# Convolution sums and inversion products in PSUM, gates on ScalarE, a shorter reciprocal root

## The chip, the cores and the metric

The kernel runs on one core of one Trainium2 chip. Its engines are TensorE (PE, with weight loads shown apart as PEld), VectorE (DVE), ScalarE (ACT), GpSimd (POOL) and SyncE (SP), which here issues DMAs; ACT issues some too. The metric is the device time of one execution in microseconds, lower is better. A run is one number; the median of several is what counts, and one execution has been recorded as a profile.

## What is computed

One encoder layer with four head groups, on two requests of 2048 tokens by 1024 features (`r` = 0 and 1) with shared weights. Cut to what matters here:

```python
def gdn_chunked(q, k, v, g, beta):              # chunks of 64 tokens, 32 of them
    l_mat = where(strict, einsum(k_beta, k) * decay, 0)
    sol = triangular_solve(eye + l_mat, rhs, lower=True, unit_diagonal=True)
    ...                                         # a scan over 32 chunks, state 64x64 per head

def gdn_branch(qkv, gates, conv_w, ...):
    act = silu(centred_dwconv(qkv, conv_w))     # 5 taps along the sequence, one filter a channel
    q, k, v = split(act, 3)
    q, k = l2_norm(q) * HEAD_DIM ** -0.5, l2_norm(k)
    ...                                         # forward and backward scan, then rms_norm

def encoder_layer(x, mem, ...):
    proj = rms_norm(x, pre_g) @ w_in
    y_a = fourier_mix(a_u, w_fnet) * silu(a_z)
    y_b = gdn_branch(b_qkv, b_gates, ...) * silu(b_z)
    y_c = neighbourhood_attn(cq, ck, cv, rpb) * silu(c_z)
    y_d = memory_attn(d_q, rms_norm(mem, mem_g), w_mem_kv) * silu(d_z)
    out = concatenate([y_a, y_b, y_c, y_d]) @ w_out
    return x + rms_norm(out, post_g)
```

## The kernel before

Products are made from pairs of 16-bit parts, three matmuls each (L484 to L486, L494 to L496, L500 to L502 are the three of one product). `build` issues the stages and gives each a band of priority; a scheduler then writes each engine's list from the bands and the dependences, with a timing model of its own, so that stages overlap. Within an engine the list is run in order.

- **Projections** (`pass_a`, `pass_b`, `pass_z`, band 0): blocks of 256 tokens are normed (`xblock`), transposed through memory (`xT`), and multiplied by the columns of `w_in` into the PSUM tile `pj`, two banks called `mm`. `pass_a` makes q, k, v for the convolution, stored as `braw`, and the gates: ACT copies 256 columns of a `pj`, and DVE copies its last 16, scaled (L569).
- **gdn_pre** (band 3): for each request and each of 8 blocks of 256 tokens, `conv_pair` runs for k, q and v, 48 pairs in all. It loads `craw`, and for each half (128 channels) ACT writes the first tap (L889) and DVE adds the other four (L891), all in the SBUF tile `cacc`; ACT makes the tanh (L893), and DVE the product (L894). ACT and POOL then split it into two parts for PE. `norms` makes the reciprocal norms of q and k by `rsqrt`. `gdn_pair` multiplies chunks (PSUM tiles `p`, of which DVE makes `kt` at L1005, `lt` and `mt` at L1013) and stores the records `rec`.
- **gdn_sub(0)**, then **gdn_sub(1)** (band 1): triangular inversions by 31 steps in two directions `d`, on two diagonal blocks `b`. Each step makes a product `pr` (L1056) and adds it to `T` (L1059); DVE does b = 1, POOL b = 0, both in SBUF. Then blocks are combined on PE (`px`, `pz`).
- **gdn_chain** (bands 1 and 1.5): the 32 steps of the scan. PE's products are called `pc` and `pw`; SP loads `rA` and others ahead of each step; `gdn_out` stores `yb`.
- **fnet** (band 2): for each request a butterfly on DVE (L1331 to L1334), DFT products on PE (`pdf`, PSUM banks `s` and `t`), and features (`pfy` on PE, `Y` on DVE at L1434 and L1438).
- **mem_attn**, then **na_attn** (band 2): memory attention, and neighbourhood attention in 64 iterations, with scores in banks `s` and `t`, transposes by DMA (`nPT`, L1639), values `pno`, stores `yc` (L1666).
- **pass_o**: the output projection `po`, 8 blocks for each request; `prep` loads `yb`, the others' results and the gate path `oz`, and DVE and POOL multiply.

PSUM has eight banks: two `mm`; `s`, `t`, `o` (pool `pat`); `ga`, `gq`, `as` (pool `pgd`, the delta rule's). SBUF pools on the right belong to gdn_pre, gdn_sub(0), gdn_sub(1) and the chain in turn, so these run one after the other.

`rsqrt` (L232) is a bit trick (a shift, L239, and a multiply-add on integers, L240) and three Newton steps of three operations (L243, L244, L245), all small and on DVE. It serves the norms of x, of q and k, of the gdn output, of the memory and of the output.

The lines of the convolution:

```python
acc = pp.tile([P, 2, CB], F32, name=self.nm("cacc"), tag="cacc", bufs=2)
for f in range(2):
    w = self.cws[:, 2 * i + f]
    nc.scalar.activation(acc[:, f], raw[:, f, 0:CB], AF.Copy, scale=w[:, 0:1])
    for t in range(1, 5):
        nc.vector.scalar_tensor_tensor(out=acc[:, f], in0=raw[:, f, t:t + CB], ...)
```

## Time and profile before

| | |
|---|---|
| runs, us | 2514.59, 2507.51, 2510.41; median 2510.41 |
| profiled execution | 2511.93 us, span from first to last instruction 2510.2 us |
[...]
| busy over the span | PE 2008.5 us (80%), DVE 1935.1 (77%), ACT 1153.7 (46%), POOL 1059.3 (42%) |
| instructions | PE 23715, DVE 4693, ACT 2530, POOL 1149 |
| DMA | 476.07 MB, 190 GB/s on average |

A share over the whole span is an average over stages with different limits. The page's slices, the busy time by stage, the waits and the single groups of instructions say more; they are in the section of rows below. An operation is named by its line in the kernel before (L891); in `out<-in` stand the names of the tiles. A wait is put down to the engine and line that released it last.

### The profile page before, as it was taken

Reading aid. Unit: us, or ns where it says so; the run is one execution under the profiler, and the core shown is the slowest. Engines: PE = TensorE matmul, PEld = TensorE weight load, DVE = VectorE, ACT = ScalarE, POOL = GpSimd, SP = SyncE. Lnnn points to the kernel's source line nnn. Section 1 sums busy time; section 2 is a strip of 40 time slices with the busy share of each in tenths; the row PEclk is TensorE's granted clock in tenths of the full one; section 3 lists DMA queues with packets and bytes.
Section 4 is the critical chain, followed back from the end, with each engine's and each line's share of the span. In section 5 each row is a group of like instructions: output and inputs, shape, how many; then the busy total and the mean of one; then the engine's idle time right before and its main releaser. Section 6 shows DMA issues by size and latency. Waiting matters only on the chain. (4 is left out here: it accounts for less than half of the span.)

```text
span 2510.2 us, 60051 instructions
## 1 busy us (share of the span) xinstructions
PE 2008.5 (80%) x23715; PEld 1711.6 (68%) x23715; DVE 1935.1 (77%) x4693; ACT 1153.7 (46%) x2530; POOL 1059.3 (42%) x1149
## 2 busy tenths in 40 slices
PE   0787778787446776899688998878877899899998
PEld 0565667666335665687566787767766888788887
DVE  3579998989999979767987857767577756677764
ACT  1455544553354421345166755657566644332322
POOL 1236665445476667613853422222223343433320
PEclk9988899887757998899899998999989999999999
DMA  9899999999745695499789987999999984555543
GB/s 89 185 203 192 205 237 234 240 205 231 170 111 145 172 226 127 110 243 181 156 178 224 213 210 214 217 194 206 231 181 231 218 264 139 172 185 184 189 158 118
DMA packets 827483, 476.07 MB, mean 190 GB/s; under 512 B 556864, under 2 KB 789952, under 8 KB 818752
## 3 DMA queue, kind: packets, MB, share of 16 engines
q1 hardware_dynamic: 802624, 438.67, 76.5%
q10 hardware_dynamic: 24576, 33.56, 4.5%
q8 instruction: 186, 3.05, 0.5%
q14 instruction: 97, 0.79, 0.1%
HBM read 243.38 MB, written 163.73 MB: 162 GB/s over the span
## 5 line engine op out<-in xcount | busy, mean ns | idle before, releaser
L484 PE MATMUL pj<-xT,w 128*128 128x256 f16 x2592 | 739.2, 285 | 131.6 <-DVE st L213 42.5
L486 PE MATMUL pj<-xT,w 128*128 128x256 f16 x2592 | 737.2, 284 | 4.5 <-POOL w L421 4.5
L485 PE MATMUL pj<-xT,w 128*128 128x256 f16 x2592 | 738.2, 285 | 0.0
L485 PEld LDWEIGHTS <-w 128*128 128x128 f16 x2592 | 264.6, 102 | 114.0 <-issue 74.5
L484 PEld LDWEIGHTS <-w 128*128 128x128 f16 x2592 | 264.2, 102 | 106.4 <-issue 32.1
L486 PEld LDWEIGHTS <-w 128*128 128x128 f16 x2592 | 264.5, 102 | 53.8 <-POOL w L421 10.5
L500 PE MATMUL po<-w,oy 128*128 128x256 f16 x1024 | 280.6, 274 | 0.8 <-ACT oy L715 0.8
L502 PE MATMUL po<-w,oy 128*128 128x256 f16 x1024 | 280.1, 274 | 1.4 <-DVE oy L716 1.4
L501 PE MATMUL po<-w,oy 128*128 128x256 f16 x1024 | 280.7, 274 | 0.0
L891 DVE SCALAR_TENSOR_TENSOR cacc<-craw,cws,cacc 128x256 f32<-128x256 f32 x384 | 241.5, 663 | 7.2 <-ACT cacc L889 5.9
L494 PE MATMUL pj<-w,xT 128*128 128x272 f16 (+1 forms) x512 | 153.5, 300 | 41.6 <-ACT st L561 23.2
L230 POOL TENSOR_TENSOR oy<-oy,oz 128x512 f32<-128x512 f32 x60 | 100.7, 1699 | 189.2 <-ACT oy L701 178.2
L1165 POOL COPY bk<-rA 64x512 f16<-64x512 f16 x124 | 84.8, 684 | 224.9 <-PE pw L502 167.1
L765 ACT ACTIVATE oj<-po,wsc_o 128x256 f32<-128x256 f32 x128 | 59.5, 470 | 244.3 <-PE po L502 244.3
L421 POOL TENSOR_TENSOR w<-wt,w 128x512 f16<-128x512 f32 (+1 forms) x70 | 85.9, 1236 | 172.6 <-ACT w L419 150.5
L495 PE MATMUL pj<-w,xT 128*128 128x272 f16 (+1 forms) x512 | 153.8, 301 | 0.8 <-POOL w L421 0.8
L496 PE MATMUL pj<-w,xT 128*128 128x272 f16 (+1 forms) x512 | 153.6, 300 | 0.0
L500 PE MATMUL pno<-nPT,nv 128*128 128x64 f16 x704 | 78.6, 200 | 62.1 <-DMA nPT<-np__2821_27987 25.3
L1172 ACT ACTIVATE b<-rA 64x1536 f16<-64x1536 f16 x64 | 92.7, 1475 | 53.0 <-PE pc L1133 30.5
L227 POOL TENSOR_TENSOR km<-kt,km 128x256 f16<-128x256 f32 x128 | 95.2, 765 | 39.3 <-ACT km L1009 37.4
L502 PEld LDWEIGHTS <-oy 128*128 128x128 f16 x1024 | 100.6, 98 | 13.7 <-DVE oy L716 1.8
L500 PEld LDWEIGHTS <-oy 128*128 128x128 f16 x1024 | 100.6, 98 | 13.0 <-ACT oy L715 0.9
(443 smaller groups left out, 6153.5 us busy)
## 6 DMA issues: line engine op xcount, KB each, us to landing
xT<-xTd SPq DMA_DIRECT2D x32, 1024.0 KB
rec<-km SPq DMA_DIRECT2D x32, 768.0 KB
rA<-rec SPq DMA_DIRECT2D x64, 384.0 KB
xTd<-xT SPq DMA_DIRECT2D x16, 1024.0 KB
sz<-st ACTq DMA_DIRECT2D x64, 256.0 KB
oz<-sz SPq DMA_DIRECT2D x16, 1024.0 KB
out_dram<-oo SPq DMA_DIRECT2D x32, 512.0 KB
craw<-braw SPq DMA_DIRECT2D x48, 260.0 KB
```

Of the source, the lines that this page charges most:

```text
L227: self.nc.gpsimd.tensor_tensor(out=out, in0=a, in1=b, op=ALU.subtract)
L230: self.nc.gpsimd.tensor_tensor(out=out, in0=a, in1=b, op=ALU.mult)
L484: nc.tensor.matmul(ps, whi, xhi, start=(kt == 0), stop=False)
L485: nc.tensor.matmul(ps, whi, xlo, start=False, stop=False)
L486: nc.tensor.matmul(ps, wlo, xhi, start=False, stop=(kt == KT - 1))
L494: nc.tensor.matmul(ps, xhi, whi, start=(kt == 0), stop=False)
L495: nc.tensor.matmul(ps, xhi, wlo, start=False, stop=False)
L496: nc.tensor.matmul(ps, xlo, whi, start=False, stop=(kt == KT - 1))
L500: nc.tensor.matmul(ps, whi, xhi, start=start, stop=False)
L501: nc.tensor.matmul(ps, whi, xlo, start=False, stop=False)
L502: nc.tensor.matmul(ps, wlo, xhi, start=False, stop=stop)
L891: nc.vector.scalar_tensor_tensor(out=acc[:, f], in0=raw[:, f, t:t + CB], scalar=w[:, t:t + 1], in1=acc[:, f], op0=ALU.mult, op1=ALU.add)
```

## The change

Four edits.

1. The convolution's sums live in a PSUM tile `pcv`, in the banks `s` and `t` in turn (a counter `ncv`); `cacc` in SBUF holds only the result of the product after the tanh.
2. In the inversions the product of b = 1, DVE's, goes to a PSUM tile `pq` in bank `as`; POOL's stays in `pr`. A switch `SPLITADD` that was always on is gone.
3. The scaled copy of the gates is made by ACT.
4. `rsqrt` has 8 operations for 11: one integer operation for two, one Newton step of three, and one step of a higher order of four.

```diff
@@ -148,7 +148,6 @@
 PSS = ("s", "t")
 PSV = ("o", "o")
 SUB = 1
-SPLITADD = lambda k: True
 
 
 class Kern:
@@ -173,6 +172,7 @@
         self.D = {}
         self.prio = {}
         self.xbufs = 2
+        self.ncv = 0
         self.zh = {}
 
     def nm(self, s):
@@ -236,13 +236,17 @@
         n = x.shape[-1]
         y = self.tt([P, n], tag=f"rq{n}", bufs=4)
         t = self.tt([P, n], tag=f"rt{n}", bufs=4)
-        nc.vector.tensor_scalar(out=y.bitcast(I32), in0=x.bitcast(I32), scalar1=1, scalar2=None, op0=ALU.logical_shift_right)
-        nc.vector.tensor_scalar(out=y.bitcast(I32), in0=y.bitcast(I32), scalar1=-1.0, scalar2=float(0x5F3759DF),
-                                op0=ALU.mult, op1=ALU.add)
-        for i in range(3):
-            eng.scalar_tensor_tensor(out=t, in0=y, scalar=-0.5, in1=y, op0=ALU.mult, op1=ALU.mult)
-            eng.scalar_tensor_tensor(out=t, in0=t, scalar=1.0, in1=x, op0=ALU.mult, op1=ALU.mult)
-            eng.scalar_tensor_tensor(out=(out if i == 2 else y), in0=t, scalar=1.5, in1=y, op0=ALU.add, op1=ALU.mult)
+        stt = lambda o, a, s, b, op: eng.scalar_tensor_tensor(out=o, in0=a, scalar=s, in1=b, op0=op, op1=ALU.mult)
+        nc.vector.tensor_scalar(out=y.bitcast(I32), in0=x.bitcast(I32), scalar1=-0.5, scalar2=float(0x5F3759DF), op0=ALU.mult, op1=ALU.add)
+        stt(t, y, -0.5, y, ALU.mult)
+        stt(t, t, 1.0, x, ALU.mult)
+        stt(y, t, 1.5, y, ALU.add)
+
+        c = math.sqrt(0.375)
+        stt(t, y, c, y, ALU.mult)
+        stt(t, t, 1.0, x, ALU.mult)
+        stt(t, t, -1.25 / c, t, ALU.add)
+        stt(out, t, 1.875, y, ALU.add)
 
     def consts(self):
         nc, I = self.nc, self.I
@@ -566,7 +570,7 @@
                 ps = self.pmm.tile([P, 512], F32, name=self.nm("pj"), tag="mm")
                 self.mm_tok(ps[:, 0:272], W["ag"], 272, xT, t * P)
                 nc.scalar.activation(st[:, t], ps[:, 0:256], AF.Copy, scale=2.0 ** -19)
-                nc.vector.tensor_scalar(out=self.gates[r][:, 2 * tb + t, :], in0=ps[:, 256:272], scalar1=d, scalar2=None, op0=ALU.mult)
+                nc.scalar.activation(self.gates[r][:, 2 * tb + t, :], ps[:, 256:272], AF.Copy, scale=d)
             nc.scalar.dma_start(D[f"au{r}"][:, 2 * tb:2 * tb + 2, :], st)
 
         def between(tb):
@@ -883,15 +887,18 @@
         i = "qkv".index(u)
         raw = pp.tile([P, 2, CB + 4], F32, name=self.nm("craw"), tag="craw", bufs=2)
         nc.sync.dma_start(raw, self.D[f"braw{r}"][:, 2 * i:2 * i + 2, tb * CB:tb * CB + CB + 4])
-        acc = pp.tile([P, 2, CB], F32, name=self.nm("cacc"), tag="cacc", bufs=2)
+
+        pcv = self.pat.tile([P, 2, CB], F32, name=self.nm("pcv"), tag="st"[self.ncv % 2])
+        self.ncv += 1
         for f in range(2):
             w = self.cws[:, 2 * i + f]
-            nc.scalar.activation(acc[:, f], raw[:, f, 0:CB], AF.Copy, scale=w[:, 0:1])
+            nc.scalar.activation(pcv[:, f], raw[:, f, 0:CB], AF.Copy, scale=w[:, 0:1])
             for t in range(1, 5):
-                nc.vector.scalar_tensor_tensor(out=acc[:, f], in0=raw[:, f, t:t + CB], scalar=w[:, t:t + 1], in1=acc[:, f], op0=ALU.mult, op1=ALU.add)
+                nc.vector.scalar_tensor_tensor(out=pcv[:, f], in0=raw[:, f, t:t + CB], scalar=w[:, t:t + 1], in1=pcv[:, f], op0=ALU.mult, op1=ALU.add)
+        acc = pp.tile([P, 2, CB], F32, name=self.nm("cacc"), tag="cacc", bufs=2)
         e = pp.tile([P, 2, CB], F32, name=self.nm("cexp"), tag="cexp", bufs=2)
-        nc.scalar.activation(e, acc, AF.Tanh, scale=self.cinv[:, i:i + 1])
-        nc.vector.scalar_tensor_tensor(out=acc, in0=e, scalar=1.0, in1=acc, op0=ALU.add, op1=ALU.mult)
+        nc.scalar.activation(e, pcv, AF.Tanh, scale=self.cinv[:, i:i + 1])
+        nc.vector.scalar_tensor_tensor(out=acc, in0=e, scalar=1.0, in1=pcv, op0=ALU.add, op1=ALU.mult)
         if u == "v":
             dst = [self.vt[:, :, l].rearrange("p n f c -> p f n c") for l in range(2)]
         else:
@@ -1044,21 +1051,19 @@
                 nc.gpsimd.memset(T[d], 0.0)
                 nc.gpsimd.memset(T[d].rearrange("p b i j -> p b (i j)")[:, :, 0:1024:33], 1.0)
             pr = tl([P, 2, 2, 256], F32, "pr")
+            pq = self.pgd.tile([P, 2, 256], F32, name=self.nm("ppr"), tag="as")
 
             for k0 in range(31):
                 for d in range(2):
                     k = k0 if d == 0 else 31 - k0
                     js, is_ = (slice(k + 1, 32), slice(0, k + 1)) if d == 0 else (slice(0, k), slice(k, 32))
                     nj, ni = js.stop - js.start, is_.stop - is_.start
-                    pv = pr[:, d, :, 0:nj * ni].rearrange("p b (j i) -> p b j i", j=nj)
+                    pv = [t.rearrange("p (j i) -> p j i", j=nj) for t in (pr[:, d, 0, 0:nj * ni], pq[:, d, 0:nj * ni])]
                     for b in range(2):
                         eng = nc.vector if b == 1 else nc.gpsimd
-                        eng.tensor_tensor(out=pv[:, b], in0=lp[d][:, b, k, js].unsqueeze(2).to_broadcast([P, nj, ni]),
+                        eng.tensor_tensor(out=pv[b], in0=lp[d][:, b, k, js].unsqueeze(2).to_broadcast([P, nj, ni]),
                                           in1=T[d][:, b, k, is_].unsqueeze(1).to_broadcast([P, nj, ni]), op=ALU.mult)
-                        if SPLITADD(k0):
-                            eng.tensor_tensor(out=T[d][:, b, js, is_], in0=T[d][:, b, js, is_], in1=pv[:, b], op=ALU.add)
-                    if not SPLITADD(k0):
-                        nc.vector.tensor_tensor(out=T[d][:, :, js, is_], in0=T[d][:, :, js, is_], in1=pv, op=ALU.add)
+                        eng.tensor_tensor(out=T[d][:, b, js, is_], in0=T[d][:, b, js, is_], in1=pv[b], op=ALU.add)
 
             lo = [tl([P, 32, 32], F32, f"lo{d}") for d in range(2)]
             for d in range(2):
```

New lines in the rows below: the first tap is L895, the sums L897, the gates L573, the inversions' products L1064 and adds L1066, the transposes L1644.

First place: ACT's list in the convolution, the first taps of two pairs (`braw`, `au` are stores of projections, `km` is gdn_pair's, `xh` a norm of x). Before:

```order
L561 ACTIVATE st_3468<-pj_3469 128x512 [waits PE_49]
L889 ACTIVATE cacc_14303<-craw_14301,cws 128x256 [waits DMAHW2_49,Pool_49]
L889 ACTIVATE cacc_14303<-craw_14301,cws 128x256
L1014 ACTIVATE km_14357<-mt_14377 128x2x2x64 [waits DVE_49]
L562 DMA braw_3153<-st_3468 128x2x256 [waits DMAHW1_49,Activation_49]
L1014 ACTIVATE km_14357<-mt_14400 128x2x2x64 [waits DVE_49]
L889 ACTIVATE cacc_14473<-craw_14471,cws 128x256 [waits DMAHW4_49,Pool_49]
L889 ACTIVATE cacc_14473<-craw_14471,cws 128x256
```

Of the changed kernel:

```order
L895 ACTIVATE pcv_13775<-craw_13773,cws 128x256 [waits DMAHW6_49]
L895 ACTIVATE pcv_13943<-craw_13941,cws 128x256 [waits DMAHW7_49]
L572 ACTIVATE st_2507<-pj_2535 128x256 [waits PE_49]
L573 ACTIVATE gates_212<-pj_2535,wsc_ag 128x16
L574 DMA au_211<-st_2507 128x512 [waits Activation_49]
L895 ACTIVATE pcv_13775<-craw_13773,cws 128x256 [waits DVE_49]
L470 ACTIVATE xh_3112<-xt_3091,ty_3100 128x1024 [waits DMAHW4_49,DVE_49]
L895 ACTIVATE pcv_13943<-craw_13941,cws 128x256 [waits DVE_49]
```

The two first taps of one pair stood together; now each pair's second stands behind other rows and waits for DVE.

Second place: DVE's list at the first inversion (`A`, `T` of L1056 or L1064 and L1066; `U`, `Z`, `R` are the butterfly of fnet(1), `Y` fnet(0)'s features). Before:

```order
L1332 TENSOR_TENSOR R_25588<-U_25544 128x128 x2
L1332 TENSOR_TENSOR Z_25587<-U_25544 128x128 [waits DVE_49]
L1331 TENSOR_TENSOR Z_25587<-U_25544 128x128
L1333 SCALAR_TENSOR_TENSOR Z_25587<-U_25544,Z_25587 128x128 [waits DVE_49]
L1333 SCALAR_TENSOR_TENSOR Z_25587<-U_25544,Z_25587 128x128
L1334 TENSOR_SCALAR Z_25587<-U_25544 128x128
L1056 TENSOR_TENSOR pr_16814<-A_1648_16792,T_1649_16797 128x31 [waits DMAHW4_49,DMAHW5_49,DMAHW0_49,Pool_49]
L1331 TENSOR_TENSOR R_25588<-U_25544 128x128 [waits DVE_49]
```

Of the changed kernel:

```order
L1439 SCALAR_TENSOR_TENSOR Y_25105<-pfy_25219,fk,fsb_25218 128x2x128 [waits Activation_49]
L1443 SCALAR_TENSOR_TENSOR Y_25105<-fsb_25218,Y_25105 128x128 [waits DVE_49]
L1443 SCALAR_TENSOR_TENSOR Y_25105<-fsb_25218,Y_25105 128x128
L1064 TENSOR_TENSOR ppr_16761<-A_1696_16738,T_1697_16743 128x31 [waits DMAHW5_49,DMAHW3_49,DMAHW6_49,DMAHW1_49,DMAHW7_49,DMAHW0_49,Pool_49]
L1066 TENSOR_TENSOR T_1697_16743<-T_1697_16743,ppr_16761 128x31 [waits DVE_49]
```

The butterfly stood around the first product; now features of fnet(0) stand there, and the butterfly comes after the first inversions.

Third place: SP's list near the end of the scan and of neighbourhood attention (`rA` loads of the scan, `nPT` and `yc` neighbourhood attention, `yb` stores of the scan's last steps). Before:

```order
L1639 DMA_TRANSPOSE nPT_32370<-np__2818_27981 128x12x128
L1639 DMA_TRANSPOSE nPT_32442<-np__2819_27983 128x12x128
L1157 DMA rA_23938<-rec_12917 128x2x384
L1295 DMA yb_2_3102<-osq_23286 128x256
L1295 DMA yb_2_3113<-osq_23289 128x256
L1161 DMA rA_23938<-recs_12916 128x2x128
L1666 DMA yc_3109<-nya_32164 256x1x256
L1639 DMA_TRANSPOSE nPT_32499<-np__2820_27985 128x12x128
```

Of the changed kernel, behind the last load of `rA`:

```order
L1644 DMA_TRANSPOSE nPT_32294<-np__2868_27905 128x12x128
L1671 DMA yc_3079<-nya_32088 256x1x256
L1644 DMA_TRANSPOSE nPT_32366<-np__2869_27907 128x12x128
L1300 DMA yb_7_3077<-osq_24952 128x256
L1644 DMA_TRANSPOSE nPT_32423<-np__2870_27909 128x12x128
L1300 DMA yb_7_3088<-osq_24955 128x256
L1300 DMA yb_0_3070<-osq_24958 128x256
L1644 DMA_TRANSPOSE nPT_32482<-np__2871_27911 128x12x128
```

Transposes of neighbourhood attention stood ahead of loads for the scan's later steps; now the last of them stand among the scan's last stores.

## Rows read from the trace of the kernel before

**Rows 1.** The page's slices (40 of 62.8 us): DVE and the DMA engines.

```profile
DVE  3579998989999979767987857767577756677764
DMA  9899999999745695499789987999999984555543
```

**Rows 2.** Busy time of each engine by stage; columns: PE, PEld, DVE, ACT, POOL, granted clock, DMA share.

```profile
120.00:870.00 750.00, 542.16 (x4837) 444.14 (x4836) 695.83 (x1734) 357.50 (x791) 412.40 (x434) 0.83 0.85 194
870.00:1435.00 565.00, 471.08 (x4946) 386.97 (x4945) 464.25 (x890) 246.48 (x527) 303.69 (x351) 0.93 0.85 184
1435.00:2125.00 690.00, 583.86 (x10336) 523.30 (x10337) 470.07 (x1357) 398.77 (x841) 212.06 (x273) 0.94 0.91 210
2125.00:2510.00 385.00, 365.56 (x3265) 321.86 (x3263) 253.84 (x515) 116.63 (x314) 109.62 (x68) 0.97 0.48 168
```

**Rows 3.** Waits from 120 to 890 us: waiter, releaser, us in total, times, longest.

```profile
ACT cexp L893 <- DVE cacc L891: 83.8, 27, 6.6
PE p L500 <- DVE mt L1013: 39.0, 24, 3.7
PE pj L484 <- DVE gates L569: 29.1, 10, 5.9
```

**Rows 4.** Tiles on PE, first and last start: the scan, neighbourhood attention, output projection.

```profile
L1130 PE MATMUL pc<-rV,b x256: 189/193/261, 1435.7 to 2087.0; 128*128 128x64 f16 x128
L1133 PE MATMUL pc<-v,b x504: 193/193/242, 1454.8 to 2100.2; 128*128 128x64 f16 x168
L500 PE MATMUL pno<-nPT,nv x704: 189/193/242, 1540.8 to 2002.4; 128*128 128x64 f16 x176
L500 PE MATMUL po<-w,oy x1024: 271/273/421, 2144.9 to 2500.0; 128*128 128x256 f16 x171
```

**Rows 5.** Groups of DVE by line and shape; xcount, busy us, mean ns, idle before.

```profile
L891 DVE SCALAR_TENSOR_TENSOR cacc<-craw,cws,cacc 128x256 f32<-128x256 f32 x384 | 241.5, 663 | 7.2 <-ACT cacc L889 5.9
L1005 DVE TENSOR_TENSOR kt<-p,ke 128x512 f32<-128x512 f32 x64 | 43.3, 681 | 3.9 <-POOL km L227 3.6
L1434 DVE SCALAR_TENSOR_TENSOR Y<-pfy,fk,fsb 128x256 f32<-128x256 f32 x12 | 7.8, 648 | 2.3 <-ACT fsb L1432 2.3
L569 DVE TENSOR_SCALAR gates<-pj,wsc_ag 128x16 f32<-128x16 f32 x32 | 7.2, 224 | 9.6 <-ACT st L568 9.4
```

**Rows 6.** Single lines: shortest, median and longest ns, first and last start, DVE and ACT.

```profile
L891 DVE SCALAR_TENSOR_TENSOR cacc<-craw,cws,cacc x384: 379/479/1580, 122.7 to 855.1; 128x256 f32<-128x256 f32 x192
L889 ACT ACTIVATE cacc<-craw,cws x96: 491/494/548, 122.1 to 844.8; 128x256 f32<-128x256 f32 x96
L1013 DVE TENSOR_TENSOR lt<-p,df x64: 402/413/425, 213.5 to 894.8; 128x256 f32<-128x256 f32 x64
```

**Rows 7.** Busy time on DVE before 900 us: lines 239, 240, 243, 244, 245 in turn.

```profile
0.00:900.00 900.00, 9.97 (x34) 0.85 0.87 189
0.00:900.00 900.00, 10.17 (x34) 0.85 0.87 189
0.00:900.00 900.00, 37.01 (x102) 0.85 0.87 189
0.00:900.00 900.00, 35.75 (x102) 0.85 0.87 189
0.00:900.00 900.00, 35.03 (x102) 0.85 0.87 189
```

**Rows 8.** Line 1059, the inversions' adds, on POOL and on DVE.

```profile
L1059 POOL TENSOR_TENSOR T<-T,pr x124: 248/660/2205, 924.3 to 1295.6; 128x31 f32<-128x31 f32 x8, 128x60 f32<-128x60 f32 x8, 128x87 f32<-128x87 f32 x8, 128x112 f32<-128x112 f32 x8
L1059 DVE TENSOR_TENSOR T<-T,pr x124: 177/413/2495, 943.8 to 1262.2; 128x31 f32<-128x31 f32 x8, 128x60 f32<-128x60 f32 x8, 128x87 f32<-128x87 f32 x8, 128x112 f32<-128x112 f32 x8
```

**Rows 9.** DVE from 900 to 936 us: line 1332, then line 1333.

```profile
900.00:936.00 36.00, 14.12 (x17) 0.95 1.24 199
900.00:936.00 36.00, 7.45 (x16) 0.95 1.24 199
```

**Rows 10.** The chain that ended last, a load ahead of the first `po`.

```profile
2138.76 7.88 DMA oz<-sz
```

## The prediction, made before the changed kernel ran

> **What bounds the kernel now.** I read the slices of the page first, then busy time by stage, then the waits inside the first stage, then the single operations the change touches.
>
> The slices show DVE between 80 and 90% or more of each slice from the fourth to the fourteenth, and the DMA engines near full there too, by digits of 9 [rows 1]. The second view cuts the span where the program's serial chain changes: the convolution and the gdn_pair work (120 to 870 us), the inversions (870 to 1435), the 32 steps of the scan (1435 to 2125), the output projection (2125 to 2510). In the first stage DVE is busy 695.83 of 750 us, PE 542.16 at a granted clock of 0.83, ACT 357.50, POOL 412.40, DMA share 0.85 [rows 2]. In the second no engine is full (PE 471.08, DVE 464.25 of 565). In the third PE leads (583.86 of 690, DMA 0.91), in the last it is PE alone (365.56 of 385). So DVE time taken out of the first stage is worth most of itself; DVE time taken out later is worth what the chain there lets through.
>
> The waits of the first stage agree: the others wait for DVE. ACT's tanh waited 83.8 us, 27 times, for the conv sums; PE waited 39.0 us for `mt` and 29.1 us for DVE's copy of the gates [rows 3].
>
> Behind it two chains run side by side. The serial one is gdn_pre, gdn_sub(0), gdn_sub(1), gdn_chain; the other is fnet, memory attention, neighbourhood attention. Both must end before the output projection, whose first `po` starts at 2144.9 us. The scan's first `pc` starts at 1435.7, its last at 2100.2 (32 steps, 20.8 us each); neighbourhood attention's last `pno` starts at 2002.4 [rows 4]. Today the scan ends last, by 98 us.
>
> **The conv sums (removes 0, changes 384 DVE operations).** L891 is 241.5 us, 663 ns on average [rows 5], but its shortest is 379, its median 479 and its longest 1580 ns [rows 6]: an operation with both tensors in SBUF is often stretched. Operations with one tensor in PSUM are not: L1013, equally 256 wide, lies between 402 and 425 with a median of 413 [rows 6], and L1005, 512 wide, averages 681 [rows 5]. None of these writes PSUM as well. I take 440 ns, near 413, the row of the same width, with a little for the write: 384 x 0.44 = 169, **-72 us**. Bounds: 413 ns gives -83; 648 ns, which L1434 takes at the same width on a PSUM operand and two from SBUF [rows 5], gives 249, +7. L894 moves one operand to PSUM too; I count nothing.
>
> [...]
>
> **What the sums add: a handshake.** `acc` was two buffers of SBUF; ACT wrote the first term of both halves back to back (order, first place), and DVE then had eight operations without a wait. Now ACT's second init stands behind DVE's work on the first half, with 1 to 19 other ACT rows between, and DVE's second half waits for that init, 48 times. On DVE's list 1 to 26 other rows (about 6 in the middle) lie between the halves, some 2 to 3 us at 0.4 us each; the init itself is 0.49 us [rows 6]. So most of the handshakes are covered. Bounds: 0, and 48 x 3.1 = 149 us, if each costs what a wait between these two engines costs now (83.8 / 27) [rows 3]. I take **+15**, 0.3 us each, nearer to 0 because of the cover; behind the waiting DVE stand all gdn_pair's `kt` and `mt`, for which PE waits.
>
> [...]
>
> **Roots.** 34 calls lie before 900 us. L239 and L240 are 9.97 and 10.17 us, L243, L244, L245 37.01, 35.75, 35.03 (102 each) [rows 7], so 352 ns on average. One of the two integer operations goes (-10.0), and two of nine of the others (34 x 2 x 0.352 = -23.9): **-34 us**. The bound below is half of it, if calls wait on ACT or PE rather than DVE. Later calls are off the full engine: 0.
>
> **Gates.** 32 operations of 224 ns [rows 5] leave DVE: **-7 us**; ACT takes at most 32 x 0.49 = 16 us (a 256 wide copy, [rows 6]), hidden as ACT is busy 357.50 of 750 [rows 2]. PE's 29.1 us behind them [rows 3] shrink, but PE is not the bound: 0.
>
> Stage 1: -72 + 15 - 34 - 7 = -98 on DVE. I let 80% through (PE busy 72% at the low clock and the DMA engines near full take the rest): **-80**. Ends of this share: half and all.
>
> **Inversions and the second stage.** DVE's half of the products is written to PSUM, so its adds read one operand there. 124 adds of 413 ns in the middle are 51 us, and by the ratio of the conv sums (0.44 for 0.663) they lose 17. But POOL's half runs until 1295.6, DVE's until 1262.2 [rows 8]: POOL's own chain ends last. I take **-10**, with 0 and -40 (POOL gains where DVE's stretch came from sharing SBUF) as bounds. The order also moves a whole thing: fnet(1)'s butterfly stood on DVE between the end of gdn_pair and the first product (second place) and now stands after the first inversions. From the last L1013 (894.8) to DVE's first add (943.8) lie 49 us [rows 6, 8]; between 900 and 936 the butterfly's two largest lines alone take 14.12 and 7.45 us of them [rows 9]. I take the 30 between the sum of these two and the whole 36: **-30**. Against it fnet(0)'s DFT, which shares banks s and t with the conv sums, is now behind the last conv pair on PE (5398 matmuls stand ahead of the first, 4613 before): its features come between DVE's first products: **+15**. Stage 2: **-25**.
>
> **The scan**: the same 10.1 thousand PE instructions between first and last `pc` in both lists: **0**; bounds -20 and +20 for other company.
>
> **The tail.** By the order, neighbourhood attention's last `pno` now stands after the scan's last `pc`: four to five iterations (64 from 1540.8 to 2002.4, 7.2 us each [rows 4]), some 35 us, remain when the scan is done (third place). Then come its `yc` stores and the loads of `oz` (7.88 us before the first `po` [rows 10]), some 30 us. Today 44.7 us lie between the last `pc` and the first `po`; 35 + 30 - 45 = **+20**. Bounds 0 and +40. The output projection is PE's: 0.
>
> **Sum**: -80 - 25 + 0 + 20 = -85 on the profiled execution's 2511.93 (span 2510.2 and 1.7 around it): 2427. That execution is 1.5 us above the median of 2510.41, so **2425 us**.
>
> **Rivals.**
> - *More than that.* All of -113 (no handshake cost) arrives, POOL speeds up with DVE, -40 for the inversions with -30 and +15 is -55: -113 - 55 + 20 = -148, 2362; with less from POOL up to 2395, 2350 to 2395. For it: others wait for DVE in all of stage 1 [rows 3]. Against: the DMA slices [rows 1]. Chance 0.12.
> - *The attention chain sets the end.* fnet can no longer run beside the convolution, memory attention then ends some 20% further into the scan, and neighbourhood attention has to run in what is left. If an iteration takes 8.0 instead of 7.2 us because transposes, scan loads and `xT` loads share DMA (0.91 in that stage [rows 2]), 64 x 0.8 = 50 us more at the end: 2425 + 45 = about 2470, 2460 to 2495. Chance 0.17.
> - *The change does not do what it says.* Sums that read and write PSUM take L1434's 648 ns: +7 + 15 - 34 - 7 = -19, 80% of it -15, with -25 and +20 a total of -20: 2490, 2480 to 2510. Chance 0.07.
> - *Slower: the handshake.* One mechanism, ACT's second init of each conv pair. If DVE waits 3.1 us at each of 48, -113 + 149 = +36 in stage 1, and -5 behind it: +31, 2541. It decides from 118 / 48 = 2.5 us a pair on. For it: ACT's list has up to 19 rows, some waiting for PE, between the inits. Against: DVE's list has work between the halves, and ACT is under half busy. Chance 0.12.
>
> **How the numbers follow.** My forecast (2395 to 2460) has 0.52. A measurement here tells 0.3%, 7.5 us, from no change. Faster: the forecast, the first two rivals and half of the third, 0.52 + 0.12 + 0.17 + 0.03 = 0.84; slower 0.11, same 0.05. The range 2355 to 2500 leaves out the handshake rival and the ends of the first and third, some 0.18.
>
> **What would show it.** Right: L891's successor near 0.44 us with a narrow spread; DVE's waits for ACT's init some 15 us in all; the last L1013 near 815 us instead of 894.8 [rows 6]; the first product directly behind; scan's start near 1330; last `pno` after last `pc`; first `po` near 2060. Wrong: sums at 0.6 us; DVE waiting over 100 us for the inits; the last `pno` over 60 us behind the last `pc`; the first stage as long as now with the DMA engines full.

## The result, and the profile after

The changed kernel takes **2394.66 us** in the median of 4 runs (2389.98 to 2395.28), the kernel before 2508.96 us on the same chip: a ratio of 0.953, 95% interval 0.9508 to 0.9551. The forecast was 2425 us with a range of 2355 to 2500, so the time lies in the range and the direction was right; the gain is 114 us where 85 were forecast. The profiled executions are 2511.93 and 2394.09 us, 117.8 apart (their spans, 2510.2 and 2392.2, are 118.0 apart); the steps below add up to that.

From the page of the changed kernel, busy time and slices:

```profile
PE 1966.7 (82%) x23715; PEld 1685.4 (70%) x23715; DVE 1803.1 (75%) x4484; ACT 1158.4 (48%) x2562; POOL 1027.3 (43%) x1149
DVE  3469978879999869968986687677787884665663
PEclk9898899999778999999989999999999997999999
DMA  9899999999756694879899999799999997545532
```

PE is still the busiest engine, and it is busy 42 us less for the same matmuls (2008.5 before). DVE's digits of slices 4 to 14 (59.8 us each) are 7 to 9, a little lower than in [rows 1]; the DMA engines' digits are as before.

Now the busy time by stage, cut at the program's own marks: the end of gdn_pair, the scan's first and last `pc`, and the first `po`. The columns are those of [rows 2]. The kernel before:

```profile
0.00:895.10 895.10, 611.97 (x5435) 501.27 (x5436) 764.35 (x1983) 401.95 (x875) 452.24 (x483) 0.85 0.87 189
895.10:1435.70 540.60, 447.11 (x4683) 365.18 (x4682) 447.49 (x843) 237.08 (x505) 286.04 (x327) 0.93 0.85 180
1435.70:2100.20 664.50, 561.77 (x10135) 503.62 (x10136) 454.70 (x1304) 388.16 (x819) 204.53 (x264) 0.94 0.93 212
2100.20:2144.90 44.70, 35.97 (x310) 30.79 (x306) 29.71 (x104) 19.99 (x39) 16.32 (x16) 0.93 0.58 184
2144.90:2510.20 365.30, 351.68 (x3162) 310.73 (x3162) 238.82 (x463) 106.56 (x296) 100.18 (x60) 0.98 0.47 165
```

The changed kernel:

```profile
0.00:830.90 830.90, 581.35 (x5379) 484.00 (x5379) 669.25 (x1814) 397.42 (x889) 428.98 (x484) 0.89 0.93 200
830.90:1326.20 495.30, 433.34 (x4553) 364.85 (x4554) 401.58 (x783) 205.11 (x406) 271.18 (x324) 0.96 0.85 188
1326.20:1965.50 639.30, 562.59 (x10124) 493.32 (x10125) 491.58 (x1367) 417.12 (x900) 206.34 (x262) 0.95 0.99 221
1965.50:2027.00 61.50, 37.44 (x503) 32.44 (x500) 28.44 (x106) 37.37 (x86) 22.71 (x22) 0.81 0.80 236
2027.00:2392.20 365.20, 352.01 (x3166) 310.76 (x3164) 212.25 (x419) 101.34 (x284) 98.13 (x59) 0.98 0.46 167
```

So the five stages changed by -64, -45, -25, +17 and 0 us. The two kernels do nearly the same matmuls in each stage; some 200 of 20,500 moved into the tail. PE's busy and idle time therefore say where the 118 us are. In the first stage PE was busy 30.6 us less for 1% fewer matmuls, at a granted clock of 0.89 instead of 0.85, and idle 33.6 us less (249.5 for 283.1). In the scan PE is busy as long as before (562.6 and 561.8) and idle 26 us less. Over the span idle time fell by 76 us and busy time by 42. The last columns show the DMA engines fuller where time was saved: a share of 0.93 in the first stage (0.87 before) and of 0.99 in the scan (0.93 before).

The lines of the edits themselves, changed kernel, shortest, median and longest ns, first and last start; behind them the group of the sums (busy us, mean ns, idle before), that of the copies to `kbd`, and the busy time of `rsqrt` on DVE before 900 us (L239, then L240):

```profile
L897 DVE SCALAR_TENSOR_TENSOR pcv<-craw,cws,pcv x384: 401/480/492, 135.1 to 780.3; 128x256 f32<-128x256 f32 x192
L895 ACT ACTIVATE pcv<-craw,cws x96: 454/477/481, 134.6 to 772.6; 128x256 f32<-128x256 f32 x96
L1020 DVE TENSOR_TENSOR lt<-p,df x64: 361/411/425, 197.0 to 830.6; 128x256 f32<-128x256 f32 x64
L1066 POOL TENSOR_TENSOR T<-T,pr x124: 246/646/1990, 854.2 to 1167.3; 128x31 f32<-128x31 f32 x8, 128x60 f32<-128x60 f32 x8, 128x87 f32<-128x87 f32 x8, 128x112 f32<-128x112 f32 x8
L1066 DVE TENSOR_TENSOR T<-T,ppr x124: 168/353/422, 857.7 to 1184.4; 128x31 f32<-128x31 f32 x8, 128x60 f32<-128x60 f32 x8, 128x87 f32<-128x87 f32 x8, 128x112 f32<-128x112 f32 x8
L573 ACT ACTIVATE gates<-pj,wsc_ag x32: 257/268/334, 99.4 to 619.5; 128x16 f32<-128x16 f32 x32
L897 DVE SCALAR_TENSOR_TENSOR pcv<-craw,cws,pcv 128x256 f32<-128x256 f32 x384 | 176.3, 480 | 17.1 <-ACT pcv L895 14.8
L981 DVE COPY kbd<-kq 64x512 f16<-64x512 f16 x64 | 39.5, 617 | 3.0 <-POOL kq L227 2.4
0.00:900.00 900.00, 75.48 (x238) 0.90 0.94 200
0.00:900.00 900.00, 11.64 (x34) 0.90 0.94 200
```

They answer to [rows 5] to [rows 8]. The conv sums take 480 ns on average, none over 492, where the mean was 663 and the longest 1580. The roots take 87.1 us where they took 127.9. POOL's adds are hardly shorter (646 ns in the middle for 660); DVE's are 353 for 413 and none over 422, where the longest was 2495.

The waits around the sums between 120 and 820 us (waiter, releaser, us, times, longest):

```profile
ACT pcv L895 <- DVE pcv L897: 54.3, 23, 7.0
DVE pcv L897 <- ACT pcv L895: 14.8, 10, 2.6
ACT cexp L900 <- DVE pcv L897: 30.1, 15, 4.7
DVE ty L464 <- ACT xq L462: 34.3, 9, 12.9
PE p L504 <- DVE mt L1020: 48.0, 18, 7.3
```

DVE waited 14.8 us for first taps, and ACT waited 54.3 us for DVE in turn; its wait before the tanh fell from 83.8 [rows 3] to 30.1. DVE's wait for `xq`, ACT's squares for the norm of x, is new in this size: 36.1 us to the end of gdn_pair where it was 11.7. PE's waits for `mt` are 48.0 us, 39.0 before [rows 3].

**What stretched the sums.** The timelines of DVE and POOL show it. Columns: start, us, engine, line, operation. Kernel before, DVE:

```profile
281.56 2.77 DVE L891 SCALAR_TENSOR_TENSOR cacc<-craw,cws,cacc 128x256 f32<-128x256 f32 x3
284.24 0.22 DVE L569 TENSOR_SCALAR gates<-pj,wsc_ag 128x16 f32<-128x16 f32 x1
284.39 2.36 DVE L891 SCALAR_TENSOR_TENSOR cacc<-craw,cws,cacc 128x256 f32<-128x256 f32 x3
286.67 1.27 DVE L811 COPY g<-gates 64x32 f32<-64x32 f32 x4
287.98 0.88 DVE L891 SCALAR_TENSOR_TENSOR cacc<-craw,cws,cacc 128x256 f32<-128x256 f32 x2
289.48 0.88 DVE L891 SCALAR_TENSOR_TENSOR cacc<-craw,cws,cacc 128x256 f32<-128x256 f32 x2
```

and POOL in the same stretch:

```profile
281.34 1.09 POOL L223 TENSOR_TENSOR csq<-csq 128x512 bf16<-128x512 f32 x1
282.38 1.66 POOL L227 TENSOR_TENSOR km<-kt,km 128x256 f16<-128x256 f32 x2
284.00 0.85 POOL L227 TENSOR_TENSOR km<-mt,km 128x256 f16<-128x256 f32 x1
284.81 1.65 POOL L227 TENSOR_TENSOR km<-kt,km 128x256 f16<-128x256 f32 x2
286.43 0.85 POOL L227 TENSOR_TENSOR km<-mt,km 128x256 f16<-128x256 f32 x1
290.31 1.16 POOL L227 TENSOR_TENSOR vt<-cacc,vt 128x512 f16<-128x512 f32 x1 [3.03 <-ACT vt L901]
```

While POOL works without a gap (281.34 to 287.28), six sums take 2.77 and 2.36 us, 0.8 to 0.9 us each. In POOL's gap behind it pairs take 0.88, 0.44 each. Changed kernel, DVE, all of it beside a busy POOL:

```profile
189.21 0.47 DVE L897 SCALAR_TENSOR_TENSOR pcv<-craw,cws,pcv 128x256 f32<-128x256 f32 x1
189.60 0.72 DVE L239 SCALAR_TENSOR_TENSOR ty<-ty 128x2 f32<-128x2 f32 x1
190.25 0.47 DVE L897 SCALAR_TENSOR_TENSOR pcv<-craw,cws,pcv 128x256 f32<-128x256 f32 x1
190.64 0.80 DVE L239 SCALAR_TENSOR_TENSOR ty<-ty,ty 128x2 f32<-128x2 f32 x1
191.37 0.48 DVE L897 SCALAR_TENSOR_TENSOR pcv<-craw,cws,pcv 128x256 f32<-128x256 f32 x1
191.76 0.92 DVE L239 SCALAR_TENSOR_TENSOR ty<-ty,ty 128x2 f32<-128x2 f32 x1
192.60 0.87 DVE L897 SCALAR_TENSOR_TENSOR pcv<-craw,cws,pcv 128x256 f32<-128x256 f32 x2
193.38 0.55 DVE L239 SCALAR_TENSOR_TENSOR ty<-ty 128x2 f32<-128x2 f32 x1
```

and its POOL:

```profile
189.16 2.27 POOL L425 TENSOR_TENSOR w<-wt,w 128x512 f16<-128x512 f32 x2
191.39 1.27 POOL L992 TENSOR_TENSOR df<-df,gmask 128x512 f32<-128x512 f32 x1
192.61 2.55 POOL L227 TENSOR_TENSOR km<-kt,km 128x256 f16<-128x256 f32 x4
```

The sums stay at 0.47 and 0.48, while the small operations of `rsqrt` between them, with all their operands in SBUF, take 0.55 to 0.92 us. Over all 384 sums of each kernel: before, 199 had hardly any work of POOL beside them (under 5% of their time) and took 475 ns on average, 486 at most; 96 had POOL at work nearly all through (over 95%) and took 949 ns on average. In the changed kernel the means of the two kinds, 175 and 156 sums, are both 480. Work of ACT or of the DMA engines beside a sum makes no such difference: its share and the duration have a correlation of 0.02 and -0.05 before (0 is none, 1 is full), POOL's one of 0.74. A sum in PSUM is no faster than an undisturbed one in SBUF (480 ns for 475); it is only never disturbed (none over 492 ns, where the longest in SBUF took 1580). So a sum with its accumulator in PSUM is not lengthened beside POOL, and one with both tensors in SBUF mostly is (84 of those 96 took over 600 ns). By what mechanism POOL's work lengthens it, no run shows. The shortest sum is 401 ns in PSUM and 379 in SBUF, 22 ns apart.

### The profile page after: what moved, and what is told of

It reads as the page before. It is cut to its first block, busy times and chain, and to the rows that moved or that the text cites. A ratio compares the mean times of both kernels' runs of the same rounds, so it can differ in the third digit from the quotient of the medians.

```text
span 2392.2 us, 59873 instructions
## 1 busy us (share of the span) xinstructions
PE 1966.7 (82%) x23715; PEld 1685.4 (70%) x23715; DVE 1803.1 (75%) x4484; ACT 1158.4 (48%) x2562; POOL 1027.3 (43%) x1149
## 4 chain that ended last, share of the span: by engine, by line
PE 32%; DVE 27%; DMA 24%; SPq 5%; issue 5%; POOL 3%; ACT 3%; ACTq 0%; DVEq 0%; POOLq 0%
PE po L505 4%; PE po L504 4%; PE po L506 4%; PE pj L490 3%; PE pj L489 3%; PE pj L488 3%; DVE pcv L897 3%; DVE ppr L1064 2%; DMA nPT<-np__2868_27905 2%; DMA nPT<-np__2869_27907 2%; DMA xT<-xh 2%; DMA rec<-km 2%; DMA w<-in_w_in_dram 2%; DVE ty L239 2%; DMA nPT<-np__2871_27911 2%
## 5 line engine op out<-in xcount | busy, mean ns | idle before, releaser
L488 PE MATMUL pj<-xT,w 128*128 128x256 f16 x2592 | 729.8, 282 | 107.9 <-DMA xT<-xh 25.7
L490 PE MATMUL pj<-xT,w 128*128 128x256 f16 x2592 | 729.2, 281 | 9.7 <-POOL w L425 9.7
L489 PE MATMUL pj<-xT,w 128*128 128x256 f16 x2592 | 729.4, 281 | 0.0
L488 PEld LDWEIGHTS <-w 128*128 128x128 f16 x2592 | 261.1, 101 | 102.9 <-issue 36.1
L489 PEld LDWEIGHTS <-w 128*128 128x128 f16 x2592 | 261.2, 101 | 91.9 <-issue 54.3
L490 PEld LDWEIGHTS <-w 128*128 128x128 f16 x2592 | 261.5, 101 | 58.6 <-POOL w L425 11.5
L897 DVE SCALAR_TENSOR_TENSOR pcv<-craw,cws,pcv 128x256 f32<-128x256 f32 x384 | 176.3, 480 | 17.1 <-ACT pcv L895 14.8
L498 PE MATMUL pj<-w,xT 128*128 128x272 f16 (+1 forms) x512 | 147.5, 288 | 28.6 <-DVE st L213 17.2
L499 PE MATMUL pj<-w,xT 128*128 128x272 f16 (+1 forms) x512 | 147.9, 289 | 0.9 <-POOL w L425 0.9
L500 PE MATMUL pj<-w,xT 128*128 128x272 f16 (+1 forms) x512 | 147.6, 288 | 0.0
L227 POOL TENSOR_TENSOR km<-kt,km 128x256 f16<-128x256 f32 x128 | 88.4, 711 | 65.7 <-ACT km L1016 59.6
L506 PEld LDWEIGHTS <-oy 128*128 128x128 f16 x1024 | 100.5, 98 | 14.4 <-DVE oy L720 2.6
L505 PEld LDWEIGHTS <-oy 128*128 128x128 f16 x1024 | 100.6, 98 | 13.2 <-issue 1.1
L504 PEld LDWEIGHTS <-oy 128*128 128x128 f16 x1024 | 100.5, 98 | 12.0
```

The lines of the kernel that those rows point to most:

```text
L227: self.nc.gpsimd.tensor_tensor(out=out, in0=a, in1=b, op=ALU.subtract)
L488: nc.tensor.matmul(ps, whi, xhi, start=(kt == 0), stop=False)
L489: nc.tensor.matmul(ps, whi, xlo, start=False, stop=False)
L490: nc.tensor.matmul(ps, wlo, xhi, start=False, stop=(kt == KT - 1))
L498: nc.tensor.matmul(ps, xhi, whi, start=(kt == 0), stop=False)
L499: nc.tensor.matmul(ps, xhi, wlo, start=False, stop=False)
```

## The experiments

The theories: A, the parts save time on DVE and the order that follows (fnet behind the convolution, memory attention beside the scan) saves the rest; B, time on DVE alone, with the later gains from the inversions; C, each kernel's list has its own luck of half a per cent.

Twelve kernels were run, in three sets of four, each set with its own runs of the kernel before (medians 2523.94, 2535.37 and 2533.58 us: slower chips than that of the result). Ratios are against these. Ends of stages are best compared within a set: mix12 has the changed kernel's list up to the end of gdn_pair, instruction by instruction, and reached it at 850.9 us, not 830.9. That is 2.4% later, while the kernel before is 1.0% slower on that chip (2533.58 for 2508.96). The whole change was not run again on those chips. An estimate from these two: slower by 2.4% over its whole length, it would have had a ratio of 0.953 x 1.024 / 1.010 = 0.967 there. So beside 0.953 the ratios of these sets don't tell differences below some 0.014.

The last three columns are the stages of the profiled execution behind gdn_pair, in us: to the scan's first `pc`, from there to its last, and from there to the first `po` (which in mix12 starts ahead of the last `pc`). The first two rows are the kernels of the result, on its faster chip; where a stage of a run is set beside before's below, it is beside this row.

| set | kernel | ratio (95% interval) | end of gdn_pair, us | inversions | scan | to first `po` |
|---|---|---|---|---|---|---|
| | before | 1 | 895.1 | 540.6 | 664.5 | 44.7 |
| | changed | 0.953 (0.9508 to 0.9551) | 830.9 | 495.3 | 639.3 | 61.5 |
| 1 | conv_only | 0.9814 (0.977 to 0.9857) | 862.4 | 513.8 | 662.2 | 80.6 |
| 1 | root_only | 1.000 (0.9974 to 1.0026) | 897.1 | 530.4 | 671.0 | 53.1 |
| 1 | inv_only | 0.9924 (0.9897 to 0.995) | 898.7 | 535.4 | 681.5 | 29.8 |
| 1 | gate_only | 1.0035 (1.0012 to 1.0059) | 900.3 | 544.9 | 668.4 | 47.1 |
| 2 | no_conv | 0.975 (0.972 to 0.9781) | 905.6 | 502.5 | 665.6 | 37.8 |
| 2 | no_root | 0.9699 (0.9661 to 0.9737) | 866.0 | 510.7 | 645.4 | 58.0 |
| 2 | no_inv | 0.9691 (0.9636 to 0.9745) | 847.1 | 509.7 | 645.2 | 91.7 |
| 2 | fnet_late | 1.0014 (0.9991 to 1.0037) | 910.6 | 511.6 | 653.3 | 96.9 |
| 3 | two_banks | 0.9649 (0.9615 to 0.9683) | 843.6 | 506.2 | 674.8 | 51.6 |
| 3 | conv_root | 0.968 (0.9643 to 0.9717) | 827.7 | 526.6 | 660.1 | 60.9 |
| 3 | root_plus | 1.001 (0.9991 to 1.0029) | 937.4 | 518.6 | 654.2 | 42.1 |
| 3 | mix12 | 0.9603 (0.9568 to 0.9639) | 850.9 | 502.0 | 814.1 | -148.3 |

**One part at a time.** Each is the kernel before with one of the four edits, word for word as in the change's diff: `conv_pair`, `rsqrt`, the loop of `gdn_sub`, the line of the gates.

> The kernel before with the convolution's sums in PSUM and nothing else. Theory A (order and time): the sums lose 65 us of DVE and wait 15, of which 60% reach the end of gdn_pre (-30), and because the pool of banks s and t now serves the convolution first, fnet falls behind it and memory attention runs beside the scan: -20 in the inversions' stage and -25 in the scan, +17 in the tail: near 2450. Theory B (time alone; the later gains come from the inversions' products): -30 and nothing later: near 2478.

> The kernel before with roots of 8 operations. Both theories: 41 us of DVE ahead of 900 us (127.9 became 87.1 in the changed kernel), 60% of it at the end: near 2484. The prediction's 80% would give 2476.

> The kernel before with DVE's half of the inversions' products in PSUM. Theory A: the adds on DVE fall from 413 to 353 ns in the middle, POOL's chain ends last all the same: 0 to -10, 2500 to 2509. Theory B: the gain of the second stage and of what follows is from here: -45, near 2464.

> The kernel before with the gates copied by ACT. Both theories: 7 us off DVE, 60% of it: near 2505, hardly told from no change. If PE's 29 us behind these copies counted, near 2485.

Conv alone gives 47 us on this chip, between the two theories. Of Theory A's terms behind gdn_pre, the inversions' stage is shorter, as it said and by more (27 us), but the scan is not (662.2 us), and the tail is 36 us longer. Conv alone ends gdn_pair 36 us ahead of the three kernels whose sums are in SBUF (897 to 900). Roots alone give nothing, against both theories. The inversions alone give 19, more than Theory A's 10 and less than half of Theory B's 45; their stage is only 5 us shorter. The gates alone are 9 us slower although DVE has 7 us less to do; why, no run shows. The four gains add up to a ratio of 0.977; the whole gave 0.953. The combinations below, on two other chips, come out under the sum of their parts too: no_conv 0.975 for 0.996, no_root 0.970 for 0.977, no_inv 0.969 for 0.985, conv_root 0.968 for 0.981. So, unless the chip of the first set is the odd one, the parts help one another.

What became of the roots' time stands in two rows, busy time to the end of gdn_pair (columns as above). Roots alone:

```profile
0.00:897.10 897.10, 601.32 (x5429) 496.02 (x5430) 751.90 (x1880) 399.40 (x873) 460.35 (x483) 0.88 0.87 188
```

Inversions alone, on the same chip, with the roots of 11 operations:

```profile
0.00:898.70 898.70, 602.21 (x5436) 495.48 (x5437) 764.44 (x1982) 401.74 (x875) 454.37 (x483) 0.86 0.88 188
```

To these ends the roots of 11 operations are 121.8 us of DVE in inv_only's trace, those of 8 are 85.0 in root_only's. Yet DVE was busy only 12.5 us less, for its operations other than roots and sums took 475.9 us for 452.5.

**One part taken back.** The changed kernel with one edit undone, the rest as it is; and, as a test of order alone, the kernel before with

```diff
-FN = 2
+FN = 3.5
```

> The changed kernel with the convolution's sums back in SBUF: roots, gates and inversions alone. If the edits add up as when each was run alone (ratios 1.000, 1.0035, 0.9924): 0.996, some 10 us faster than before. If roots and gates are worth something only once the sums have left SBUF, the same 0.996, and the two kernels that leave out roots or inversions carry the difference. If instead the three help one another without the sums: near 0.975.

> The changed kernel with the roots of 11 operations. The whole change gave 0.953. If roots are worth nothing here either, as alone: 0.953. If they are worth their 41 us once DVE no longer waits on the shared memory: the end of gdn_pre near 860 and 0.967.

> The changed kernel with both halves of the inversions' products in SBUF. Alone this edit gave 0.9924. If it adds up: 0.961. If more, because it sits on the path only when memory attention no longer stands beside the inversions: 0.970 and the end of px later by 30 us.

> The kernel before with one number changed, the band of fnet from 2 to 3.5: the same work in another order, fnet and with it memory attention later (memory attention's first product 7185 matmuls in for 6700, neighbourhood attention's last 19734 for 18844). If the order alone carries the gain behind gdn_pre: 0.980 to 0.985, the inversions' stage 20 us shorter and the scan 25. If not: 1.00.

The order alone gives nothing in total, so the theory that fnet's later place carries the gain falls. It does move time: the inversions' stage is 29 us and the scan 11 us shorter than before's, and a first stage 15 us and a tail 52 us longer take that back. Without the sums in PSUM the other three still give 2.5%, the branch of the expectation in which they help one another without the sums; their gain lies behind gdn_pair, whose end (905.6) is hardly ahead of fnet_late's (910.6). With the sums in PSUM short roots move that end: no_inv stands 19 us ahead of no_root, and the inversions play no part there yet; no_root's 866.0 and 0.970 are near the branch in which the roots count. no_inv's 0.9691 is the figure of the branch with a late end of `px`: from the end of gdn_pair to the last `px` it took 470.7 us, 17 more than the changed kernel's 453.7, not 30. What leaving out roots (0.017) or the inversions (0.016) costs beside the whole's 0.953 is of the size of the doubt above.

**Pairs, a doubled cost, and two tries to be faster.** conv_root is conv_only with the short roots. root_plus is the kernel before with

```diff
-        for i in range(3):
+        for i in range(4):
```

in `rsqrt` (and the result written in the fourth step). two_banks is the changed kernel with

```diff
-        pcv = self.pat.tile([P, 2, CB], F32, name=self.nm("pcv"), tag="st"[self.ncv % 2])
+        pcv = [self.pat.tile([P, CB], F32, name=self.nm("pcv"), tag=g) for g in "st"]
...
+        for f in range(2):
+            nc.scalar.activation(e[:, f], pcv[f], AF.Tanh, scale=self.cinv[:, i:i + 1])
+            nc.vector.scalar_tensor_tensor(out=acc[:, f], in0=e[:, f], scalar=1.0, in1=pcv[f], op0=ALU.add, op1=ALU.mult)
```

and mix12 is the changed kernel with

```diff
-        gemm, scan, mix = 0, 3, 2
+        gemm, scan, mix = 0, 3, 1.2
```

> The changed kernel with the two halves of a conv pair in a bank each, so that the second first tap does not wait for the first half's sums; tanh and product are by halves, 48 more operations on ACT and on DVE. Theory: the handshake cost what the trace of the changed kernel shows, 14.8 us of DVE, and this gains about 15 - 8 = 7 us of them: 0.950. If the handshake's real price was more (ACT waited 54 us for DVE, and others behind it): 0.935 and the end of gdn_pre 25 us earlier. If a list that ends the attention just before the scan is worth more than that, it shows between the last pc and the first po.

> The kernel before with the sums in PSUM and the short roots, and neither gates nor inversions. Conv alone gave 0.9814, roots alone 1.000. Theory A, small operations count once the sums are off the shared memory: 0.966 to 0.970 with the end of gdn_pre 20 us earlier than conv alone. Theory C, each kernel's list of instructions has its own luck of half a per cent either way: roots alone had bad luck, and this lies at 0.970 to 0.975 with the end of gdn_pre where the roots' 15 to 20 us put it. If roots are worth nothing without the inversions: 0.981.

> The kernel before with a fourth Newton step, 14 operations a root: 34 x 3 x 0.35 = 36 us more of DVE ahead of the end of gdn_pre. If DVE's small operations bound that stage as predicted: 29 us later, ratio 1.010 to 1.012. If they slip into time that DVE loses anyway (roots alone gave 0): 1.000, end of gdn_pre as before.

> The changed kernel with one number changed, the band of memory and neighbourhood attention from 2 to 1.2: neighbourhood attention's last product stands 17522 matmuls in for 20462, and the output projection starts before the scan has ended. If the 61 us between the last pc and the first po can be filled by it: 30 to 60 us less, 0.930 to 0.941. If the scan, now with more attention beside it, grows by as much: 0.953.

conv_root's 0.968 is what Theory A expected, 0.013 better than conv alone, where the roots alone were worth 0; its interval reaches into Theory C's range, though, and the two ran on different chips. The busy time decides more than the ratio does. Its busy time to the end of gdn_pair:

```profile
0.00:827.70 827.70, 588.57 (x5475) 489.10 (x5476) 643.22 (x1847) 392.65 (x857) 425.31 (x485) 0.91 0.96 202
```

DVE is busy 643 us there against 689.0 to the same point in conv_only (another chip), 46 less and not 12.5; the roots take 72.1 us for 118.4, and the operations other than roots and sums 446.8 for 448.6. With the sums in SBUF, then, most of the roots' time was lost again to other operations, and with the sums in PSUM it was kept. Luck of half a per cent for each list (Theory C) could make up the gates' 9 us, but not this, nor the whole. Why the small operations' time was lost so fully in the kernel before is not settled: root_plus ends gdn_pair 27 and 32 us later than the two kernels of the second set with SBUF sums (910.6 and 905.6; a chip with nearly the same median), so adding to the roots does cost in that stage, and still its total is 1.001. Behind its longer first stage all is shorter:

```profile
0.00:937.40 937.40, 611.28 (x5547) 504.94 (x5548) 787.96 (x2101) 401.48 (x877) 460.78 (x484) 0.87 0.86 183
937.40:1456.00 518.60, 437.89 (x4583) 357.01 (x4582) 437.85 (x821) 233.71 (x498) 276.54 (x325) 0.94 0.86 182
1456.00:2110.20 654.20, 559.15 (x10125) 500.87 (x10126) 467.55 (x1331) 393.40 (x823) 207.85 (x265) 0.94 0.93 216
```

The second stage is 22 us and the scan 10 shorter than before's on a slower chip: matmuls of the projections (filler for PE) that ran in the longer first stage were not left for later (5547 matmuls by its end, not 5435).

two_banks ends gdn_pair 7.3 us ahead of mix12, which has the handshake: the theory's 7 us, but not by its mechanism. DVE still waited 21.9 us for first taps (10.1 in mix12), now behind the previous pair's product, and what fell was its busy time, 650.8 us for 669.2. mix12 fills the tail as meant, but the scan grows to 814 us from its first to its last `pc` (639 in the changed kernel), and it comes to 0.9603. Both ratios (0.9649 and 0.9603) are above 0.953, but by no more than the doubt above, so whether either beats the change on the same chip is not shown.

## Why the prediction was right, and which terms were off

- **Bound.** Right: gdn_pre was DVE's, and the sums leaving SBUF were the largest part. The mechanism was in the argument (an operation with both tensors in SBUF is often stretched) without its cause, POOL's work beside it (949 ns a sum, 475 without); a stretch from sharing SBUF with POOL stands only among the bounds of the inversions.
- **Conv sums, -72.** Measured -65: 241.5 to 176.3 us of busy time. 480 ns each for the 440 taken; the spread went as forecast. (The sum took 384 durations from a busy time, in which neighbours that overlap count once; 176.3 us are 459 ns a sum.)
- **Handshake, +15.** Measured 14.8, 0.3 us a pair where the slower rival needed 2.5. Whether DVE's longer waits for `xq` belong to its price is open: they are 28 to 41 us in the kernels with the sums in PSUM, but 31 us in no_conv as well.
- **Roots, -34; gates, -7.** In the changed kernel -41 for the roots. Gates -7, and 268 ns each on ACT.
- **80% of it at the end, -80.** This step failed in size: -64. The edits took 104 us off DVE (-65 - 41 - 7, and 9 more of waits for first taps, 14.8 for 5.9 [rows 5]), and 62% of that reached the end. Nor was it PE or the DMA engines that took the rest: DVE was busy only 95 us less (669.3 for 764.4), as other operations with all operands in SBUF took more, the copies to `kbd` 39.5 us for 27.3; and it was idle 31 us more (161.7 for 130.7), 9 of them the first taps and 24 its waits for `xq`.
- **Second stage, -25.** Measured -45. In the trace it is the inversions that shrank: from POOL's first add to the last add of either engine it was 371 us and is 330, so -41, where -10 was taken with -40 as the bound; all else in the stage changed by -4, where -30 and +15 were taken. "POOL's own chain ends last" no longer holds: DVE ends at 1184.4, POOL at 1167.3. POOL's second inversion, from its first product to its last add, took 124.9 us and takes 95.7, and that is the work of the edit: 94 to 96 us in all six kernels with DVE's product in PSUM, 117 to 129 in the eight with it in SBUF. It is not that POOL's operations got faster (77.3 us of products and adds, 73.8 now): POOL waits less in between (22.5 us, 4.7 now) and does less other work (25.6, 17.7 now). DVE takes longer for its part (87.4, 109.4 now), which gives some of it back. How the -45 divides between this edit and the order stays open: alone, the inversions' edit shortened the stage by 5 us, and the order of conv_only or fnet_late, without that edit, by 27 and 29.
- **The scan, 0.** Measured -25, all of it PE's idle time (102.7 to 76.7 us), with the same matmuls. The step failed; that the lists hold equally many PE instructions doesn't tell how long PE waits between them. PE's waits for neighbourhood attention's transposes are 62 us before and 45 after, but no run here isolates what shortened them, and this stays open. The scan is short in no_root and no_inv too (645 us) and not in no_conv (666); in fnet_late, where the order alone was changed, it is 653, but in root_plus 654.
- **The tail, +20.** Measured +17. The last `pno` now starts 27.5 us behind the last `pc`, and PE then waited 12.8 us for loads of `yb` and 7.8 for the gate path. Right for the new kernel; of the old one the 44.7 us were mostly PE at work on filler (36.0 us busy), which the prediction hadn't said.
- **Rivals.** The attention chain does set the first `po` now, at the price foreseen in the tail and not at 45 us. The change does what it says.
- **Luck.** The scan was forecast to start near 1330 us and the last `lt` (L1013) near 815; they came at 1326.2 and 830.6. The first is a hit by two errors that cancel, 16 us too much gain taken in the first stage and 20 too little in the second. That the profiled gain is 118 us and not the forecast 85 is, after this, mostly the scan's 25.

## What to carry to other kernels

An accumulator that DVE reads and writes many times is worth a PSUM bank where POOL works beside it on SBUF (here 480 ns a sum for 663): look for a wide gap between the shortest and the mean duration of one line (379 and 663 ns of L891), and for a narrow spread at the lines with an operand in PSUM (402 to 425 ns at L1013). Gains of such edits need not add up (a ratio of 0.977 from the four alone, 0.953 from the whole, on different chips); after one, what was worthless alone can count (shorter roots took 12.5 us off DVE's busy time to the end of gdn_pair with the sums in SBUF, 46 with them in PSUM), so price small DVE operations in the kernel in which the stretch is gone. And where one engine's list is filled with movable work, a stage that gets longer or shorter says little (root_plus ended gdn_pair 27 and 32 us later than two kernels with SBUF sums, and its ratio was 1.001); count that engine's idle time over the whole span.

## What was not expected of the hardware

PE took 108.1 ns for a matmul of the first stage (581.35 us for 5379) where it had taken 112.6 (611.97 for 5435). The granted clock there is 0.89 of full speed instead of 0.85 (over the span 0.934 instead of 0.912), a mean over its two levels: the lower one, half of full speed, was granted for 178 us of the stage and for 263 before, while PE's idle time fell from 283 to 250 us. So 24 of the 30.6 us by which PE was busy less are faster matmuls, and the rest are fewer. And the same list of instructions took 830.9 us to the end of gdn_pair on one chip and 850.9 on another, so that stages from different chips can't be compared to a per cent.
